# A two-layer trunk on one core: the stick-breaking stage gets a deeper pipeline, a half-height query tile and a GpSimd scaling

## The chip, the core and the metric

The program runs on one core of a Trainium2 chip, in one launch. What counts is the device time in microseconds (us). Before the change it is 1318.02 us, the median of 3 runs (1313.18, 1318.02 and 1321.62). The engines are TensorE (PE in the profile, with its weight loads as PEld), VectorE (DVE), ScalarE (ACT), GpSimd (POOL) and SyncE (SP), which issues most transfers.

## What is computed

The model has two layers on a sequence of 512 tokens of width 1024, all in float32. Layer 0 mixes with a gated delta net, layer 1 with stick-breaking attention; both also attend to 256 memory rows, and both end in an MLP. The change lies in two places: the stick-breaking attention of layer 1, and the softmax of the memory attention of both layers.

```python
def stick_breaking_attention(q, k, v):          # 12 heads of 64
    ...
        z = einsum('bthd,bshd->bhts', q[:, t0:t1], kb) * scale
        log_beta = log_sigmoid(z)
        log_1m_beta = where(before, log_sigmoid(-z), 0.0)
        tail = cumsum(log_1m_beta, axis=3, reverse=True) - log_1m_beta
        a = where(before, exp(log_beta + tail), 0.0)
        outs.append(einsum('bhts,bshd->bthd', a, vb))

def memory_attention(q, mem_kv):                # 4 heads of 64, 256 memory rows
    ...
    p = softmax(einsum('bshd,bmhd->bhsm', q, k) * X_HEAD_DIM ** -0.5, axis=-1)
    return einsum('bhsm,bmhd->bshd', p, v)
```

## The kernel before, in words

Every float32 matrix product is done with numbers that are split into a high part (fp32r) and the remainder, the low part; hi·hi, hi·lo and lo·hi are added up in one PSUM bank. ACT usually makes the high part by a copy, and DVE the low part by a subtraction (`split_lo`, L176).

The stick-breaking stage of layer 1 runs over *units*. A unit is one head and one entry of `BLOCKS = ((3, 2), (1,), (0,))`, that is one or two blocks of 128 keys against all queries that come later. There are 12 heads in 6 pairs, so 36 units; the two heads of a pair run one unit apart. `stick_breaking` is a generator that emits, in step n, the scores of unit n, the weights of unit n-`d1` and the value pass of unit n-`d2`:

- `sb_qk` projects query and key of a head in one product (128 output rows: 64 of q, 64 of k). From the PSUM bank ACT writes `qh` (q high, into both halves of the 128 partitions) and k high into the lower half of `kk`; DVE writes q low into both halves of `ql`, two instructions of 64x512 (L1075), and k low into the upper half of `kk`.
- `sb_scores` makes z in a bank `ps_g` by three products per block: `kk` with `qh` (L1092: k low and k high with q high in one pass over 128 rows), a mask (L1093, bf16), and `kk` with `ql` (L1095, also over 128 rows). ACT then forms log(1 + exp(-|z|)) in three instructions (L1100 to L1102), DVE adds max(z, 0) (L1103) and splits into `sp_h` (L1107) and `sp_l` (L176).
- `sb_weights` adds the reversed running sums to z by products of triangular and all-ones matrices with `sp_h` and `sp_l` (L1122). ACT takes exp into `sb_a` (L1125), DVE copies the high part `sb_ah` (L1128), and GpSimd subtracts for the low part `sb_al` (L1129).
- `sb_av` multiplies v with `sb_ah` and `sb_al` in a bank `ps_acc` (L1141), and folds the result into `mixT` when a head is complete.

Between the units the generator's caller places slices of the next pair's projection (`fm_slices`, L212) and, by the table `FILLN`, steps of `mem_attention`. There `scores` takes 256 tokens of one head at a time: two pairs of products (L691), a maximum on DVE (L694), two exponentials on ACT (L698), a reciprocal (L700) and the scaling of `p` by it, two instructions of 128x256 (L702); `turn` transposes `p` on PE (L711) and `values` multiplies with the memory values (L722). In layer 0 the same `mem_attention` is woven into the end of the delta net.

Each engine does its instructions strictly in the order in which they stand; the order comes from the framework's scheduler, which works on the emitted program, and from the pools: a new tile of a name with `bufs=k` waits until the one k before it has been read. The PSUM banks `ps_g` and `ps_acc` are four each.

Of the kernel before, what the change touches and what calls it, by code (L numbers as in the profile page):

```python
# [9 lines left out]
F32R = mybir.dt.float32r  # L10
I32 = mybir.dt.int32
BF16 = mybir.dt.bfloat16
AF = mybir.ActivationFunctionType
ALU = mybir.AluOpType
# [3 lines left out]
P = 128  # L18
S = 512
NT = S // P  # L20
D = 1024
# [3 lines left out]
W = H * DH  # L25
# [17 lines left out]
def f(ap):  # L43
    return ap.bitcast(F32)
# [23 lines left out]
class Trunk:  # L68
# [600 lines left out]
    def mem_attention(self, i, q, alloc, mixT):  # L669

        nc, v = self.nc, self.nc.vector
# [14 lines left out]
        def scores(h, t2):  # L686
# [14 lines left out]
            for j in range(2):  # L701
                v.tensor_scalar(out=p[:, j], in0=p[:, j], scalar1=sm[:, j:j + 1], scalar2=None, op0=ALU.mult)  # L702
# [359 lines left out]
    def sb_qk(self, pair, hi, lo, pool, out):  # L1062

        nc, v = self.nc, self.nc.vector
        top, low = slice(0, 64), slice(64, P)
        for hh in range(2):
            qh, ql, kk = (pool.tile([P, S], F32R, name=f"sb{n}", bufs=4) for n in ("qh", "ql", "kk"))
            out[hh] = (qh, ql, kk)

            def done(b):  # L1070
                nc.scalar.activation(out=qh[top], in_=b[top], func=AF.Copy, scale=0.125)
                nc.scalar.activation(out=kk[low], in_=b[low], func=AF.Copy)
                nc.scalar.activation(out=qh[low], in_=b[top], func=AF.Copy, scale=0.125)
                for o in (top, low):
                    v.scalar_tensor_tensor(out=ql[o], in0=b[top], scalar=0.125, in1=f(qh[top]), op0=ALU.mult,  # L1075
                                           op1=ALU.subtract)
                self.split_lo(kk[top], b[low], kk[low])
            yield from self.fm_slices(self.a["w_b_qk"][2 * pair + hh], hi, lo, done)

    def sb_scores(self, u, pool):  # L1080

        nc, v = self.nc, self.nc.vector
        qh, ql, kk = u["qk"][u["pr"].start // 64]
        u["zb"] = zb = self.bank("g")
        n = 0
        u["at"] = {}
        for i in u["blocks"]:
# [7 lines left out]
            nc.tensor.matmul(z, lhsT=kk[:, ks], rhs=ql[:, t0:], start=False, stop=True, skip_group_check=True)  # L1095
# [16 lines left out]
    def sb_weights(self, u, pool):  # L1112
# [13 lines left out]
        u["ah"] = pool.tile([P, S], F32R, name="sb_ah", bufs=2)[:, :n]  # L1126
        u["al"] = pool.tile([P, S], F32R, name="sb_al", bufs=2)[:, :n]
# [20 lines left out]
    def stick_breaking(self, qks, vv, pool, mixT):  # L1148
# [10 lines left out]
        d1, d2 = 2, 4  # L1159
# [173 lines left out]
def _qk_heads(w):  # L1333

    q, k = w[:, :W].reshape(D, 2 * H, 64), w[:, W:2 * W].reshape(D, 2 * H, 64)
    return np.concatenate([np.concatenate([q, k], 2).reshape(D, 2 * W), w[:, 3 * W:]], 1)
# [32 lines left out]
```

## Time and profile before

| | us |
|---|---|
| median of 3 runs | 1318.02 |
| the profiled execution, its own time | 1318.39 |
| span of that execution in the trace | 1316.7 |
| around the span | 1.7 |
| DVE busy / ACT busy / POOL busy | 861.8 / 717.5 / 163.9 |
| stick-breaking stage, first scores to last value pass | about 762 to 926 |

The page gives PE as busy for 97% of the span, but the ends of matmuls are modelled: a matmul of 512 columns is shown as 0.39 us long while the next begins 0.23 us after it. A busy PE therefore hides short stalls, and its idle time is a lower bound of what it loses. Stretches of time are read with the busy time of each engine in them; the stage of the change is cut at 833 us, where the memory attention of layer 1 has begun and PE stops being busy without a gap.

### The profile page before, as it was taken

To read this page: it belongs to the slowest core of one execution; us is meant where nothing else is said; L and a number is where in the kernel's file an instruction comes from. 1 tells how busy PE (TensorE), PEld (TensorE's weight loads), DVE (VectorE), ACT (ScalarE), POOL (GpSimd) and SP (SyncE) were. 2 spreads that over 40 slices of the span, in tenths; PEclk is the share of its full clock that TensorE was granted. 3 is DMA by queue.
4 is the path that set the end of the run, shared out by engine and by line. 5 is a ranking of instruction groups with operands and counts; after the bars stand their busy time and mean duration, and the time that the engine had idled before them with its cause. 6 is when DMAs were issued, how large, how long until landed. Compare 5 with 4: busy or idle time off the path is not lost.

```text
span 1316.7 us, 18097 instructions
## 1 busy us (share of the span) xinstructions
PE 1275.9 (97%) x6620; PEld 1070.0 (81%) x6620; DVE 861.8 (65%) x1588; ACT 717.5 (54%) x1378; POOL 163.9 (12%) x196
## 2 busy tenths in 40 slices
PE   7999999998999999999999999998999999999997
PEld 7788878887788888878888988786788888878886
DVE  7677695877663264555788678999573255455776
ACT  8654435446455454444565567878455344454561
POOL 2511313010021000000000013223130000000000
PEclk9999999999999999999999999999999999999999
DMA  7551654415689878644454426222679944544441
GB/s 242 192 166 58 161 130 117 123 51 143 210 245 266 233 190 243 195 145 143 148 186 139 157 75 150 76 64 64 208 255 256 257 127 144 148 141 150 152 144 64
DMA packets 82153, 209.39 MB, mean 159 GB/s; under 512 B 6720, under 2 KB 11840, under 8 KB 81616
## 3 DMA queue, kind: packets, MB, share of 16 engines
q1 hardware_dynamic: 62192, 164.12, 37.7%
q0 software_dynamic: 19296, 43.06, 16.4%
q8 instruction: 52, 0.85, 0.3%
q10 hardware_dynamic: 576, 1.05, 0.2%
q14 instruction: 37, 0.30, 0.1%
HBM read 199.29 MB, written 67.63 MB: 203 GB/s over the span
## 4 chain that ended last, share of the span: by engine, by line
PE 80%; DVE 10%; ACT 6%; issue 2%; DMA 1%; POOL 0%; SPq 0%; DVEq 0%; POOLq 0%; ACTq 0%
PE ps_acc L212 45%; PE ps_g L955 21%; PE ps_g L212 4%; PE ps_g L526 1%; PE ps_g L1122 1%; DVE wlo L176 1%; PE ps_g L389 1%; PE ps_g L518 1%; ACT whi L199 1%; PE ps_g L488 1%; ACT scrap L281 1%; DVE cv L360 1%; PE ps_g L295 1%; DVE sb_e L1103 1%; PE ps_acc L1141 1%
## 5 line engine op out<-in xcount | busy, mean ns | idle before, releaser
L212 PE MATMUL ps_acc<-h_hi,whi 128*128 128x512 f32 (+1 forms) x888 | 338.1, 381 | 0.0
L212 PE MATMUL ps_acc<-h_hi,wlo 128*128 128x512 f32 (+1 forms) x888 | 337.5, 380 | 0.0
L212 PE MATMUL ps_acc<-h_lo,whi 128*128 128x512 f32 (+1 forms) x888 | 335.1, 377 | 0.0
L176 DVE TENSOR_TENSOR wlo<-raw,whi 128x1024 fp32r<-128x1024 f32 x134 | 169.2, 1264 | 141.3 <-ACT whi L199 133.9
L955 PE MATMUL ps_g<-whi,sh 128*128 128x512 f32 x784 | 261.1, 395 | 0.0
L199 ACT ACTIVATE whi<-raw 128x1024 fp32r<-128x1024 f32 x134 | 141.8, 1059 | 203.0 <-PE ps_g L955 94.1
L176 DVE TENSOR_TENSOR wlo<-xc,whi 128x1024 fp32r<-128x1024 f32 x89 | 108.8, 1224 | 151.2 <-ACT whi L199 149.0
L212 PEld LDWEIGHTS ps_acc<-h_hi,wlo 128*128 128x128 f32 x888 | 167.5, 189 | 34.0 <-DVE wlo L176 3.9
L212 PEld LDWEIGHTS ps_acc<-h_hi,whi 128*128 128x128 f32 x888 | 167.8, 189 | 28.8 <-ACT whi L199 1.6
L212 PEld LDWEIGHTS ps_acc<-h_lo,whi 128*128 128x128 f32 x888 | 167.9, 189 | 28.4
L955 PEld LDWEIGHTS ps_g<-whi,sh 128*128 128x128 f32 x784 | 147.6, 188 | 34.5
L199 ACT ACTIVATE whi<-xc 128x1024 fp32r<-128x1024 f32 x89 | 94.3, 1060 | 137.1 <-PE ps_g L955 92.5
L955 PE MATMUL ps_g<-wlo,sh 128*128 128x512 f32 x392 | 154.8, 395 | 0.0
L955 PEld LDWEIGHTS ps_g<-wlo,sh 128*128 128x128 f32 x392 | 73.9, 189 | 17.2
L882 POOL DMA_DIRECT2D sum<-w_down x56 | 51.5, 1332 | 181.8 <-DMA sum<-w_down 104.4
L176 DVE TENSOR_TENSOR sh<-ua,sh 128x512 fp32r<-128x512 f32 x98 | 66.7, 685 | 4.7 <-ACT sh L936 4.7
L1129 POOL TENSOR_TENSOR sb_al<-sb_a,sb_ah 128x384 fp32r<-128x384 f32 (+1 forms) x36 | 41.2, 1144 | 154.8 <-DVE sb_ah L1128 133.1
L936 ACT ACTIVATE sh<-ua 128x512 fp32r<-128x512 f32 x98 | 59.9, 618 | 0.3
L212 PE MATMUL ps_acc<-ua 128*128 128x512 f32 x224 | 57.3, 391 | 0.0
L978 POOL DMA_DIRECT2D ua<-park x4 | 2.3, 574 | 388.6 <-DVE sh L176 381.2
L212 PEld LDWEIGHTS ps_acc<-ua 128*128 128x128 f32 x224 | 42.0, 188 | 8.9
L212 PE MATMUL ps_acc<-whi,h_hi 128*128 128x256 f32 (+1 forms) x144 | 44.5, 326 | 0.0
(352 smaller groups left out, 2148.2 us busy)
## 6 DMA issues: line engine op xcount, KB each, us to landing
sum<-w_down POOLq DMA_DIRECT2D x56, 512.0 KB, 9.9
xc<-w_up SPq DMA_DIRECT2D x38, 512.0 KB, 3.9
xc<-w_down SPq DMA_DIRECT2D x30, 512.0 KB, 3.9
xc<-sum SPq DMA_DIRECT2D x29, 512.0 KB, 4.0
sum<-w_down SPq DMA_DIRECT2D x28, 512.0 KB, 6.5
sum<-sum SPq DMA_DIRECT2D x28, 512.0 KB, 5.4
raw<-w_in_a SPq DMA_DIRECT2D x27, 512.0 KB, 3.8
raw<-sum SPq DMA_DIRECT2D x27, 512.0 KB, 3.7
```

Source lines behind the costliest of these rows:

```text
L176: self.nc.vector.tensor_tensor(out=lo, in0=src, in1=f(hi), op=ALU.subtract)
L199: self.nc.scalar.activation(out=hi, in_=raw, func=AF.Copy)
L212: self.nc.tensor.matmul(out, lhsT=l, rhs=r, start=start and k == 0 and i == 0, stop=stop and k == n - 1 and i == 2)
L281: nc.scalar.activation(out=self.scrap(m), in_=x[:, j * m:(j + 1) * m], func=AF.Square, accum_out=ssq[:, j:j + 1])
L295: op = nc.tensor.transpose(b[:, j, i * P:(i + 1) * P], xs[i][:, (kc + j) * P:(kc + j + 1) * P], self.ident)
L360: nc.vector.scalar_tensor_tensor(out=acc[:, j:], in0=b[:, :S - j], scalar=w[:, 3 - j:4 - j], in1=acc[:, j:], op0=ALU.mult, op1=ALU.add)
L389: self.nc.tensor.transpose(tp[:, t], src(t), self.ident)
L488: nc.tensor.matmul(sb[:, j], lhsT=self.sel[:, s4 + j], rhs=ud, start=True, stop=True)
L882: self.tc.keep_in_program_order(nc.gpsimd.dma_start(out=dst, in_=src, accum_op=ALU.add))
L936: nc.scalar.activation(out=s[:, 0], in_=src, func=AF.Copy)
L955: nc.tensor.matmul(y[t], lhsT=l, rhs=r, start=new and d == 0 and z == 0 and m == 0, stop=d == nd - 1 and z == 1 and m == 2, skip_group_che ...
L1129: nc.gpsimd.tensor_tensor(out=u["al"], in0=a, in1=f(u["ah"]), op=ALU.subtract)
```

## The change

Three edits are made, and the layout of the weights follows one of them.

- The value pass of a unit comes five steps behind its scores, not four (`d2`), and `sb_ah` and `sb_al` have three buffers each, not two.
- A pair's two heads share one tile `ql`: one head uses the upper 64 partitions, the other the lower ones. For the second head of a pair q and k change places in the weight's columns. The low part is written once, not twice, and the third product of the scores runs over 64 rows of `kk` and `ql` (`kk[kp, ks]`), where it ran over 128. Two pairs' `ql` tiles are kept, where four heads' were, so the memory that this frees is what the third `sb_ah` and `sb_al` take.
- The scaling of `p` in the memory attention (L702, both layers) is issued on GpSimd, not on DVE.

```diff
             for j in range(2):
-                v.tensor_scalar(out=p[:, j], in0=p[:, j], scalar1=sm[:, j:j + 1], scalar2=None, op0=ALU.mult)
+                nc.gpsimd.tensor_scalar(out=p[:, j], in0=p[:, j], scalar1=sm[:, j:j + 1], scalar2=None, op0=ALU.mult)
...
-        top, low = slice(0, 64), slice(64, P)
+        halves = slice(0, 64), slice(64, P)
+        ql = pool.tile([P, S], F32R, name="sbql", bufs=2)
         for hh in range(2):
-            qh, ql, kk = (pool.tile([P, S], F32R, name=f"sb{n}", bufs=4) for n in ("qh", "ql", "kk"))
-            out[hh] = (qh, ql, kk)
+            qh, kk = (pool.tile([P, S], F32R, name=f"sb{n}", bufs=4) for n in ("qh", "kk"))
+            qs, ks = halves[hh], halves[1 - hh]
+            out[hh] = (qh, ql[ks], kk, ks)
...
-                nc.scalar.activation(out=qh[top], in_=b[top], func=AF.Copy, scale=0.125)
-                nc.scalar.activation(out=kk[low], in_=b[low], func=AF.Copy)
-                nc.scalar.activation(out=qh[low], in_=b[top], func=AF.Copy, scale=0.125)
-                for o in (top, low):
-                    v.scalar_tensor_tensor(out=ql[o], in0=b[top], scalar=0.125, in1=f(qh[top]), op0=ALU.mult,
-                                           op1=ALU.subtract)
-                self.split_lo(kk[top], b[low], kk[low])
+                nc.scalar.activation(out=qh[qs], in_=b[qs], func=AF.Copy, scale=0.125)
+                nc.scalar.activation(out=kk[ks], in_=b[ks], func=AF.Copy)
+                nc.scalar.activation(out=qh[ks], in_=b[qs], func=AF.Copy, scale=0.125)
+                v.scalar_tensor_tensor(out=ql[ks], in0=b[qs], scalar=0.125, in1=f(qh[qs]), op0=ALU.mult,
+                                       op1=ALU.subtract)
+                self.split_lo(kk[qs], b[ks], kk[ks])
...
-            nc.tensor.matmul(z, lhsT=kk[:, ks], rhs=ql[:, t0:], start=False, stop=True, skip_group_check=True)
+            nc.tensor.matmul(z, lhsT=kk[kp, ks], rhs=ql[:, t0:], start=False, stop=True, skip_group_check=True)
...
-        u["ah"] = pool.tile([P, S], F32R, name="sb_ah", bufs=2)[:, :n]
-        u["al"] = pool.tile([P, S], F32R, name="sb_al", bufs=2)[:, :n]
+        u["ah"] = pool.tile([P, S], F32R, name="sb_ah", bufs=3)[:, :n]
+        u["al"] = pool.tile([P, S], F32R, name="sb_al", bufs=3)[:, :n]
...
-        d1, d2 = 2, 4
+        d1, d2 = 2, 5
...
     q, k = w[:, :W].reshape(D, 2 * H, 64), w[:, W:2 * W].reshape(D, 2 * H, 64)
-    return np.concatenate([np.concatenate([q, k], 2).reshape(D, 2 * W), w[:, 3 * W:]], 1)
+    qk = np.stack([q, k], 2)
+    qk[:, 1::2] = qk[:, 1::2, ::-1].copy()
+    return np.concatenate([qk.reshape(D, 2 * W), w[:, 3 * W:]], 1)
```

The order of instructions changes with it. First DVE, between two units of the fourth pair's time, before the change (the output's name stands left of the arrow, its inputs right of it; the numbers tell buffers apart):

```order
L1075 SCALAR_TENSOR_TENSOR sbql_8115<-ps_acc_8123,sbqh_8114 64x512 x2
L176 TENSOR_TENSOR sbkk_8116<-ps_acc_8123,sbkk_8116 64x512
L700 RECIPROCAL sm_8233<-sm_8233 128x2
L1128 CAST sb_ah_8266<-sb_a_8264 128x512
L702 TENSOR_SCALAR p_8234<-p_8234,sm_8233 128x256 x2
L1103 SCALAR_TENSOR_TENSOR sb_e_8247<-ps_g_8240,sb_e_8247 128x384
```

The same place on DVE with the change (its lines are two to four further down in the file):

```order
L1077 SCALAR_TENSOR_TENSOR sbql_8100<-ps_acc_8109,sbqh_8101 64x512
L176 TENSOR_TENSOR sbkk_8102<-ps_acc_8109,sbkk_8102 64x512
L700 RECIPROCAL sm_8215<-sm_8215 128x2
L1130 CAST sb_ah_8248<-sb_a_8246 128x512
L1148 TENSOR_TENSOR mixT_7144<-ps_acc_8048,sb_o_8254 64x512
L1105 SCALAR_TENSOR_TENSOR sb_e_8229<-ps_g_8222,sb_e_8229 128x384
```

One write of `sbql` and both scalings of `p` are gone from between the reciprocal and the next unit's `sb_e`; a fold into `mixT` has moved there. They stand now on GpSimd, whose queue before held only the subtractions for `sb_al` in this place:

```order
L1131 TENSOR_TENSOR sb_al_8188<-sb_a_8185,sb_ah_8187 128x384
L702 TENSOR_SCALAR p_8216<-p_8216,sm_8215 128x256 x2
L1131 TENSOR_TENSOR sb_al_8249<-sb_a_8246,sb_ah_8248 128x512
L1131 TENSOR_TENSOR sb_al_8297<-sb_a_8294,sb_ah_8296 128x384
L1131 TENSOR_TENSOR sb_al_8342<-sb_a_8339,sb_ah_8341 128x384
```

So the subtraction for `sb_al_8249` now stands behind two scalings that wait for the reciprocal on DVE. Last PE, the weights of one unit in the bank `ps_g_8681` and that unit's value pass (`sb_ah_8801`), before the change; rows in between that belong to other work are left out:

```order
L1122 MATMUL ps_g_8681<-sp_l2_8694,nones_r_332 128x128
L1122 MATMUL ps_g_8727<-sp_h0_8736,ntri_r_334 128x512
L1122 MATMUL ps_g_8780<-sp_h1_8789,ntri_r_334 128x384
L1141 MATMUL ps_acc_8900<-sb_ah_8801,v_6723 128x128
L1141 MATMUL ps_acc_8900<-sb_al_8802,v_6723 128x128
```

And the same with the change (bank `ps_g_8658`, value pass of `sb_ah_8778`):

```order
L1124 MATMUL ps_g_8658<-sp_l2_8671,nones_r_332 128x128
L1124 MATMUL ps_g_8707<-sp_h0_8716,ntri_r_334 128x512
L1124 MATMUL ps_g_8757<-sp_h1_8766,ntri_r_334 128x384
L1124 MATMUL ps_g_8798<-sp_h2_8810,ntri_r_334 128x128
L1143 MATMUL ps_acc_8916<-sb_ah_8778,v_6723 128x128
```

Between a unit's weights and its value pass there were the weights of two other units, and there are three now.

## Rows read from the trace of the kernel before

**Rows 1.** The page's first line.

```profile
span 1316.7 us, 18097 instructions
```

**Rows 2.** Busy time by stretch: stretch, length, each engine's busy us (instructions), granted clock, DMA.

```profile
762.00:833.00 71.00, 71.00 (x390) 59.89 (x389) 59.22 (x95) 53.88 (x99) 17.69 (x17) 1.00 0.48 121
833.00:926.00 93.00, 84.40 (x475) 68.04 (x474) 87.75 (x167) 73.08 (x161) 29.55 (x27) 1.00 0.22 56
```

**Rows 3.** Waits from 833 to 926 us: who waited for whom, us, times, longest.

```profile
PE ps_acc L1141 <- DVE sbkk L176: 2.3, 2, 1.2
PE ps_acc L1141 <- POOL sb_al L1129: 1.7, 3, 0.8
...
PE ps_acc L1141 <- DVE sb_ah L1128: 0.4, 2, 0.2
```

**Rows 4.** The chain of waits from 833 to 926 us, its shares by line.

```profile
by line: issue 9.5%; DVE sb_e L1103 8.1%; DVE sp_l L176 7.4%; DVE sp_h L1107 7.3%; DVE p L702 4.4%; ACT sb_e L1101 3.7%; ACT p L698 3.7%; ACT whi L199 3.6%; POOL sb_al L1129 3.6%; ACT sb_e L1100 3.6%; DVE sb_ah L1128 3.6%; PE ps_g L1122 3.5
```

**Rows 5.** DVE's groups from 833 to 926 us: busy us, mean ns of one, idle before.

```profile
L176 DVE TENSOR_TENSOR sp_l<-sb_e,sp_h 128x384 fp32r<-128x384 f32 x14 | 10.9, 778 | 0.2
...
L702 DVE TENSOR_SCALAR p<-p,sm 128x256 f32<-128x256 f32 x14 | 6.9, 532 | 0.1
L1075 DVE SCALAR_TENSOR_TENSOR sbql<-ps_acc,sbqh 64x512 fp32r<-64x512 f32 x10 | 6.8, 680 | 0.2
...
L1107 DVE CAST sp_h<-sb_e 128x384 fp32r<-128x384 f32 x14 | 6.4, 457 | 0.2
```

**Rows 6.** GpSimd's groups from 833 to 926 us, then one of the whole run.

```profile
L1129 POOL TENSOR_TENSOR sb_al<-sb_a,sb_ah 128x384 fp32r<-128x384 f32 x15 | 16.0, 1069 | 34.0 <-DVE sb_ah L1128 25.6 <-PE ps_acc L1141 3.7 <-ACT p L698 3.2
L1129 POOL TENSOR_TENSOR sb_al<-sb_a,sb_ah 128x512 fp32r<-128x512 f32 x8 | 10.8, 1350 | 30.4 <-DVE sb_ah L1128 30.4
...
L510 POOL MEMSET Q<- 128x256 f32 x18 | 6.9, 422 | 139.9 <-PE ps_g L526 137.0 <-DVE X L527 3.0
```

**Rows 7.** Timeline around 769 and 789 us, DVE and POOL: start us, length us, instruction.

```profile
769.85 0.56 DVE L176 TENSOR_TENSOR sp_l<-sb_e,sp_h 128x384 fp32r<-128x384 f32 x1
...
788.86 0.35 DVE L1107 CAST sp_h<-sb_e 128x384 fp32r<-128x384 f32 x1
789.24 1.58 DVE L176 TENSOR_TENSOR sp_l<-sb_e,sp_h 128x384 fp32r<-128x384 f32 x1
...
789.11 1.30 POOL L1129 TENSOR_TENSOR sb_al<-sb_a,sb_ah 128x512 fp32r<-128x512 f32 x1 [6.55 <-PE ps_acc L212]
```

**Rows 8.** The third product of the scores (L1095): all of it, then by stretch (PE, PEld).

```profile
L1095 PE MATMUL ps_g<-sbql,sbkk x48: 274/391/480, 762.7 to 910.2; 128*128 128x128 f32 x12, 128*128 128x256 f32 x12, 128*128 128x384 f32 x12, 128*128 128x512 f32 x12
...
833.00:926.00 93.00, 10.25 (x26) 5.19 (x26) 1.00 0.22 56
```

**Rows 9.** PE's timeline, around 763 us and around 284 us.

```profile
762.60 0.22 PE L1092 MATMUL ps_g<-sbqh,sbkk 128*128 128x128 f32 x1
762.66 0.23 PE L1093 MATMUL ps_g<-nmask,diag_bf 128*128 128x128 bf16 x1
762.70 0.30 PE L1095 MATMUL ps_g<-sbql,sbkk 128*128 128x128 f32 x1
762.85 0.33 PE L1092 MATMUL ps_g<-sbqh,sbkk 128*128 128x256 f32 x1
...
763.26 0.40 PE L212 MATMUL ps_acc<-h_hi,whi 128*128 128x512 f32 x1
763.49 0.39 PE L212 MATMUL ps_acc<-h_lo,whi 128*128 128x512 f32 x1
...
284.35 1.03 PE L389 MATMUL ps_g<-ident,X 128*128 128x128 f32 x8
285.14 0.37 PE L691 MATMUL ps_acc<-mk0h,qm 128*128 128x256 f32 x1
```

**Rows 10.** Layer 0's memory attention: a stretch, L702 alone on DVE, and its waits.

```profile
310.00:320.00 10.00, 8.38 (x56) 7.06 (x56) 7.73 (x23) 6.98 (x27) 0.61 (x1) 1.00 0.18 54
...
280.00:320.00 40.00, 4.88 (x16) 0.91 0.42 93
...
PE ps_acc L711 <- DVE p L702: 2.2, 3, 1.3
```

More of the change, by code (lines that the diff above doesn't have):

```diff
@@ L1082, in sb_scores @@
         nc, v = self.nc, self.nc.vector
-        qh, ql, kk = u["qk"][u["pr"].start // 64]
+        qh, ql, kk, kp = u["qk"][u["pr"].start // 64]
         u["zb"] = zb = self.bank("g")
```

## The prediction, made before the change was run

> **What bounds the kernel now.** I read first the busy time by stretch, then the waits in the stretch that loses time, then the chain of waits there, and last the groups of DVE and GpSimd. From 762 to 833 us PE is busy for the whole 71.00 us: this half of the stick-breaking stage is bound by PE, and nothing that DVE is spared can shorten it [rows 2]. From 833 to 926 us PE is busy for 84.40 of 93.00 us, so it idles for 8.6, while DVE is busy for 87.75 (94%) and ACT for 73.08 (79%). The reader is to see that DVE comes closest to being full there. The chain of waits agrees: the DVE lines that it names take 8.1 + 7.4 + 7.3 + 4.4 + 3.6 = 30.8% of the stretch, the ACT lines 3.7 + 3.7 + 3.6 + 3.6 = 14.6%, and PE's own work hardly shows [rows 4]. The gain is to be looked for in these 93 us, a fourteenth of the run, and its ceiling there is about the 8.6 us of idle PE.
>
> **DVE is spared.** Two things leave it in this stretch. The scaling of `p`, 14 instructions, is 6.9 us; of 10 writes of `ql` half go, 3.4 of 6.8 us [rows 5]. Together that is 10.3 us.
>
> **GpSimd is loaded, and DVE pays part of it.** The scaling has not run on GpSimd, so I bound it. A memset of 128x256, which only writes, took 0.422 us. The two forms of `sb_al`, with two inputs each, took 1.069 and 1.350 us for 384 and 512 columns; that is 0.28 us per 128 columns, so 256 columns would take 0.79 [rows 6]. One input lies between; I take 0.6, so 14 x 0.6 = 8.4 us (5.9 to 11.1). GpSimd is busy for 29.55 of the 93 us [rows 2] and has room. But a GpSimd instruction holds up DVE: `sp_l` of 128x384, which began 0.13 us after `sb_al`, took 1.58 us and ended 0.41 us after it [rows 7]. Early in the stage, with GpSimd idle, the same instruction took 0.56. On average it takes 0.778, and `sp_h` 0.457 against 0.35 with GpSimd idle [rows 5, 7]. That is 14 x 0.22 + 14 x 0.107 = 4.6 us lost to 26.8 us of `sb_al`, 0.17 us per us. The new scalings then cost DVE 8.4 x 0.17 = 1.4 us; the bounds are nothing and, were DVE to stand for all of their time, 11.1.
>
> **What of that reaches the end.** `p` alone is 4.4% of the chain, 4.1 us. Of the rest of DVE's work about a third is on the chain (30.8% of 93 is 28.6 us, of 87.75 busy), so `ql` brings 3.4 x 0.33 = 1.1 and the lost time takes 1.4 x 0.33 = 0.5. That makes 4.7 us. ACT, which gets no relief, is next: in the proportion of the two engines' shares of the chain, 30.8 to 14.6, I keep 68%, **3.2 us**.
>
> **The value pass one unit later.** PE waits at the value pass for `sb_al` 1.7 us in 3 waits and for `sb_ah` 0.4 us, never longer than 0.8 us at a time [rows 3]. The 48 score products span 147 us for 36 units [rows 8], so one unit more is 4.1 us of slack, and these **2.1 us** go. It also covers the new neighbours on GpSimd's queue, where a subtraction now stands behind two scalings (1.2 us) that wait for DVE's reciprocal. The 2.3 us at the same line that end with DVE's `sbkk` are a wait for a PSUM bank, not for the weights; they stay. What is late next is PE's wait for `sp_l`, whose distance (`d1`) does not change.
>
> **The narrower third product.** 48 products now run over 64 rows, between neighbours over 128, so TensorE changes its row setting 96 times: 44 times before 833 us, where each hundredth would show, and 52 times after [rows 8]. No row shows such a change. Below: the third product takes 0.15 us for 128 columns until the next starts, the first 0.06, because its weights' load is not hidden behind the mask's 0.04; if 64 rows saved that 0.09, the gain would be 4.3 us. Above: a matmul of 512 columns is shown as 0.40 us long and the next starts 0.23 after it; emptying the array each time would cost 0.17, 16 us in all. The nearest row is a change of kind: 8 transposes and then a product of another type take 0.79 us, 0.10 each as within a run, so that change is free [rows 9]. I take **zero**. The Trainium skill says otherwise (TensorEngine Tiling (Array Packing), Key Properties): a change of the tiling mode, not merely of the tile, drains the TensorE; no run here shows it, and by that rule the sum would come out as in the first rival below.
>
> **Work with one answer.** In layer 0, 16 scalings move off DVE (4.88 us), which is 77% busy where PE idles for 1.6 of 10 us; each then takes 0.3 us longer on a path on which PE already waited 2.2 us for `p` [rows 10]. The two cancel; I take zero, and 3 us either way for the range. ACT issues what it did. The shared `ql` tile is written while its pair's forerunner is finished with it, since both heads' last scores stand on PE ahead of the projection that fills it; were that not so, DVE would wait for one unit. The exchanged columns carry the same bytes in the same transfers. GpSimd's transfers (the sums for the MLP) now stand behind scalings, a few us later than before and far ahead of their readers. The third buffer costs no other tile its room.
>
> **Sum.** 3.2 + 2.1 = 5.3 us less than the profiled execution. That took 1318.39 us (span 1316.7 [rows 1] and 1.7 around it), 0.4 above the median, so 1313.1, or **1313** against the runs. Chance 0.45, own range 1306 to 1317.
>
> **Rivals.**
> - *Row settings cost.* Each of the 96 changes empties the array, 0.17 us. Before 833 us, where PE has no idle time, 44 x 0.17 = 7.5 us come on top. After it 52 x 0.17 = 8.8 us of new PE time fill the 8.6 of idle, so that the relief brings nothing. That is 1318.4 + 7.5 = **1326**, slower than before. It decides from 5.3 / 44 = 0.12 us per change if the later ones hide, and from 5.3 / 96 = 0.055 if none does. For it speaks that no product of the kernel has had fewer than 128 rows, and the page named above; against it that a change of kind is free [rows 9]. Chance 0.25.
> - *GpSimd takes it back.* The scalings take 0.79 us and DVE stands for all of it: 11.1 us against 10.3 spared. Only the later value pass is left, 2.1 us: **1316**. For it: the 1.58 us of `sp_l` [rows 7]. Against: on average 0.17, not 1. Chance 0.15.
> - *All idle time goes.* DVE was the only cause; 8.6 us in the stretch and 1.6 in layer 0 [rows 10]: 10.2 less, **1308**. For it: 94% of DVE [rows 2]; against: ACT stays at 79%, and the bank and `sp_l` waits stay. Chance 0.10.
> - *It does not do what it says.* The waits at the value pass are for banks, and ACT takes DVE's place at once: **1318**. Chance 0.05.
>
> **Range and chances.** One per cent is 13 us, about what a measurement of this kernel can tell from no change (its three runs lie 8.4 us apart). The range runs from 1304, the case that all idle goes less the 3 us that layer 0 may bring, to 1327, just above the row-setting case. Faster by over 1% (below 1304.8) needs more than all idle time of the stretch, or stalls that the modelled matmuls hide: 0.10. Slower by over 1% (above 1331.2) needs the row changes to cost more than an emptied array, the weights' load for instance: 0.09. Within 1%: 0.81.
>
> **What would show it.** Right: from 833 us to the end of the stage 5 us fewer, PE idle there about 3 us; DVE below 90%; waits for `sb_al` and `sb_ah` at the value pass gone, those for banks and `sp_l` left; no DVE group L702. The row settings are seen in the timeline where the third product follows the mask and where the next product follows it: starts 0.04 and 0.15 us later (128 columns) mean no price. GpSimd's share is seen in the mean of its L702 group, 0.6 us, and in `sp_l` and `sp_h`, which should stay near 0.8 and 0.46. I am wrong if the half before 833 us gets longer, or if the later half keeps its length although DVE is free.

## The result: 1.2% slower, and the profile after

The changed kernel takes **1334.92 us**, the median of 6 runs (1334.49 to 1337.40), against 1320.74 for the kernel before on the same chip, again of 6 runs. The ratio, estimated from all these runs, is **1.0117**, 95% interval 1.0098 to 1.0135 (the two medians alone give 1.0107). The forecast was 1313, with a range to 1327; it is wrong in size and in sign. The profiled execution spans 16.1 us more than the one before [rows 1], the first line of the page after:

```profile
span 1332.8 us, 18120 instructions
```

Where these 16.1 us lie is read from landmarks. The row below is the MLP's product L955 of the changed kernel; the two times at the end are its first and last start. Before they were 465.5 and 1297.3 us.

```profile
L955 PE MATMUL ps_g<-whi,sh x784: 389/393/404, 472.2 to 1313.4; 128*128 128x512 f32 x196
```

So 6.7 us are lost before the first L955, that is in layer 0 (two kernels below that change nothing there still come 3 us later than the kernel before, so this number is good to some 3 us). From the first scores (762.6 before, 769.3 after) to the last start of a value pass (925.5 and 941.7) the stick-breaking stage takes 172.4 us, where it took 162.9: **9.5 us more**. Behind it nothing differs (371.8 and 371.7 us to the last L955).

**The stick-breaking stage.** Busy time by stretch of the changed kernel, in the columns of [rows 2]:

```profile
769.00:840.00 71.00, 70.91 (x352) 56.20 (x351) 51.06 (x79) 49.80 (x89) 16.41 (x16) 1.00 0.41 104
840.00:942.00 102.00, 96.93 (x510) 76.34 (x509) 87.61 (x154) 78.62 (x172) 47.97 (x44) 1.00 0.21 57
```

PE is as full as before in the first 71 us and issues 352 instructions in them, not 390. In the rest its idle time has gone down, from 8.6 to 5.1 us, and DVE is 86% busy and no longer 94%; yet the stretch is 9 us longer, because the 71 us ahead of it now hold fewer blocks. So the halves are better cut at the same block. These rows count the last 26 of the 48 blocks of scores by their first product, in the kernel before and in the changed one, with the first and last start:

```profile
L1092 PE MATMUL ps_g<-sbqh,sbkk x26: 221/337/477, 833.1 to 909.9; 128*128 128x384 f32 x7, 128*128 128x512 f32 x7, 128*128 128x128 f32 x6, 128*128 128x256 f32 x6
L1094 PE MATMUL ps_g<-sbqh,sbkk x26: 220/384/474, 847.0 to 924.6; 128*128 128x384 f32 x7, 128*128 128x512 f32 x7, 128*128 128x128 f32 x6, 128*128 128x256 f32 x6
```

The first 22 blocks take 77.7 us (769.3 to 847.0), where they took 70.5: **7.2 us more**, with PE idle for no more than 0.1 us. From there to the last value pass it is 94.7 us, where it was 92.4: 2.3 more. The larger part of the loss lies where PE was full before.

In the later part PE has become the bound too, which the chain of waits from 840 to 942 us says at once (shares by line; before, the lines of DVE led it [rows 4]):

```profile
by line: PE ps_acc L212 19.6%; PE ps_g L1124 12.3%; PE ps_acc L1143 6.6%; issue 6.3%; PE ps_g L1097 4.8%; DVE sb_e L1105 4.1%; DVE sp_l L176 4.1%; POOL sb_al L1131 3.3%; DVE sp_h L1109 3.0%; PE ps_g L1094 2.7%; ACT p L698 2.4%; ACT sb_e L11
```

What PE does longer stands in its timeline at the first two blocks of scores (start, length, instruction), which answers to [rows 9]:

```profile
769.30 0.22 PE L1094 MATMUL ps_g<-sbqh,sbkk 128*128 128x128 f32 x1
769.37 0.23 PE L1095 MATMUL ps_g<-nmask,diag_bf 128*128 128x128 bf16 x1
769.53 0.32 PE L1097 MATMUL ps_g<-sbql,sbkk 64*128 64x128 f32 x1
769.78 0.38 PE L1094 MATMUL ps_g<-sbqh,sbkk 128*128 128x256 f32 x1
770.00 0.23 PE L1095 MATMUL ps_g<-nmask,diag_bf 128*128 128x128 bf16 x1
770.16 0.38 PE L1097 MATMUL ps_g<-sbql,sbkk 64*128 64x256 f32 x1
770.47 0.50 PE L212 MATMUL ps_acc<-h_hi,whi 128*128 128x512 f32 x1
770.81 0.39 PE L212 MATMUL ps_acc<-h_lo,whi 128*128 128x512 f32 x1
```

From mask to narrow product it is 0.16 us, where it was 0.04; from the narrow product of 128 columns to the next one 0.25, where it was 0.15; and the product behind that is itself late in releasing its successor (770.00 - 769.78 = 0.22 against 0.17, 770.81 - 770.47 = 0.34 against 0.23). Two blocks and the first product after them take 1.51 us, where they took 0.89: **0.31 us for each block**. With 48 blocks that is 14.9 us, or 0.155 for each of 96 changes; 22 blocks make 6.8 of it, about the 7.2 that the first part is longer.

**Layer 0.** The 16 scalings on GpSimd (duration in ns as minimum, median and maximum, then first and last start), and the wait for them that PE has at the transposes:

```profile
L702 POOL TENSOR_SCALAR p<-p,sm x16: 913/925/1448, 293.7 to 320.6; 128x256 f32<-128x256 f32 x16
```

```profile
PE ps_acc L711 <- POOL p L702: 5.7, 8, 1.5
```

On DVE one took 0.346 us, 16 were issued within 19.4 us (293.7 to 313.1), and PE waited 2.2 us for them in 3 waits [rows 10]. Now one takes 0.925, the 16 stretch over 26.9 us, 7.5 more, and PE waits at each of the 8 units.

### The profile page after: what moved, and what is told of

Its sections match the earlier page's. It is cut to its first block, busy times and chain, and to the rows that moved or that the text cites. A ratio compares the mean times of both kernels' runs of the same rounds, so it can differ in the third digit from the quotient of the medians.

```text
span 1332.8 us, 18120 instructions
## 1 busy us (share of the span) xinstructions
PE 1291.5 (97%) x6620; PEld 1076.2 (81%) x6620; DVE 850.8 (64%) x1544; ACT 719.0 (54%) x1378; POOL 196.4 (15%) x228
## 3 DMA queue, kind: packets, MB, share of 16 engines
q0 software_dynamic: 19296, 43.06, 16.1%
## 4 chain that ended last, share of the span: by engine, by line
PE 83%; DVE 8%; ACT 4%; issue 2%; POOL 1%; DMA 1%; DVEq 0%; POOLq 0%; ACTq 0%
PE ps_acc L212 46%; PE ps_g L955 21%; PE ps_g L212 4%; PE ps_g L1124 2%; PE ps_g L518 1%; PE ps_g L526 1%; PE ps_g L389 1%; DVE wlo L176 1%; ACT whi L199 1%; PE ps_g L1097 1%; PE ps_acc L1143 1%; PE ps_g L488 1%; POOL p L702 1%; PE ps_g L295 1%; DVE cv L360 1%
## 5 line engine op out<-in xcount | busy, mean ns | idle before, releaser
L212 PE MATMUL ps_acc<-h_hi,whi 128*128 128x512 f32 (+1 forms) x888 | 338.8, 382 | 0.1
L212 PE MATMUL ps_acc<-h_hi,wlo 128*128 128x512 f32 (+1 forms) x888 | 337.1, 380 | 0.0
L212 PE MATMUL ps_acc<-h_lo,whi 128*128 128x512 f32 (+1 forms) x888 | 335.1, 377 | 0.0
L955 PE MATMUL ps_g<-whi,sh 128*128 128x512 f32 x784 | 261.1, 395 | 0.0
L212 PEld LDWEIGHTS ps_acc<-h_hi,wlo 128*128 128x128 f32 x888 | 167.5, 189 | 34.0 <-DVE wlo L176 3.6
L212 PEld LDWEIGHTS ps_acc<-h_hi,whi 128*128 128x128 f32 x888 | 167.8, 189 | 30.2 <-ACT whi L199 1.6
L212 PEld LDWEIGHTS ps_acc<-h_lo,whi 128*128 128x128 f32 x888 | 167.9, 189 | 28.1
L955 PEld LDWEIGHTS ps_g<-whi,sh 128*128 128x128 f32 x784 | 147.6, 188 | 34.5
L955 PE MATMUL ps_g<-wlo,sh 128*128 128x512 f32 x392 | 154.8, 395 | 0.0
L955 PEld LDWEIGHTS ps_g<-wlo,sh 128*128 128x128 f32 x392 | 73.9, 189 | 17.2
L212 PE MATMUL ps_acc<-ua 128*128 128x512 f32 x224 | 57.2, 391 | 0.0
L212 PEld LDWEIGHTS ps_acc<-ua 128*128 128x128 f32 x224 | 42.0, 188 | 8.9
L212 PE MATMUL ps_acc<-whi,h_hi 128*128 128x256 f32 (+1 forms) x144 | 44.5, 326 | 0.0
```

Source lines behind the costliest of these rows:

```text
L212: self.nc.tensor.matmul(out, lhsT=l, rhs=r, start=start and k == 0 and i == 0, stop=stop and k == n - 1 and i == 2)
L955: nc.tensor.matmul(y[t], lhsT=l, rhs=r, start=new and d == 0 and z == 0 and m == 0, stop=d == nd - 1 and z == 1 and m == 2, skip_group_che ...
```

## The experiments

Theory **T1** after this reading: two prices, the row changes of TensorE (0.31 us a block) and the scaling on GpSimd in layer 0, less what the change recovers in the stage. The rivals: GpSimd caused all of it, the clock did, the narrow product is not dearer, the fifth unit costs by itself. Ratios are to the kernel before, run on the same chip in turn; one thousandth is 1.3 us. The runs of one kernel spread with TensorE's granted clock: the kernel before took 1313.04 us in a run with a mean clock of 0.999 and 1319.59 in one with 0.993, so a thousandth of the clock is worth about 1 us (an estimate). Where two kernels differ in it, the text says so.

| kernel | edit in short | median us | ratio, 95% interval |
|---|---|---|---|
| changed kernel | | 1334.92 | 1.0117, 1.0098 to 1.0135 |
| x1 | before + narrow product | 1325.87 | 1.0051, 1.0030 to 1.0071 |
| x2 | before + scaling on GpSimd | 1326.84 | 1.0049, 1.0030 to 1.0068 |
| x3 | before + lo parts written once | 1317.75 | 0.9988, 0.9974 to 1.0001 |
| x4 | changed, four units | 1334.51 | 1.0111, 1.0091 to 1.0131 |
| x5 | changed, layer 0 on DVE | 1326.48 | 1.0058, 1.0039 to 1.0076 |
| x6 | changed, both layers on DVE | 1326.18 | 1.0049, 1.0031 to 1.0067 |
| x7 | changed, narrow products side by side | 1332.18 | 1.0104, 1.0084 to 1.0123 |
| x8 | x6 with four units | 1329.21 | 1.0069, 1.0049 to 1.0090 |
| x9 | before + half of layer 0's scalings on GpSimd | 1318.64 | 0.9991, 0.9979 to 1.0003 |
| x10 | no third product, four units | 1307.88 | 0.9917, 0.9903 to 0.9930 |
| x11 | no third product, five units | 1313.83 | 0.9952, 0.9933 to 0.9971 |
| x12 | x3 with x9 | 1318.40 | 0.9999, 0.9983 to 1.0015 |

### x1: the narrow product alone

```diff
-            nc.tensor.matmul(z, lhsT=kk[:, ks], rhs=ql[:, t0:], start=False, stop=True, skip_group_check=True)
+            nc.tensor.matmul(z, lhsT=kk[64:, ks], rhs=ql[64:, t0:], start=False, stop=True, skip_group_check=True)
```

> The kernel before, with one edit: the third score product of each of the 48 blocks contracts over the 64 rows of the key hi part alone (it leaves out the product of the two lo parts, nothing else). Theory T1 (the changed kernel lost time in two places: about 0.31 us of TensorE per 128-64-128 row change, and the scaling on GpSimd in layer 0): 22 blocks lie in the stretch in which PE is never idle, 22 x 0.31 = 6.8 us; the 26 of the later stretch add 26 x 0.31 = 8.1 us, less what fits into PE's 8.6 us of idle time there. So 7 to 12 us slower, 1324 to 1329 against 1317, and no change before the first scores. Rival R1 (GpSimd and its contention with VectorE caused the whole loss): no change, within 2 us. Rival R2 (the narrower product is cheaper): up to 4 us faster.

Measured 1.0051, that is 6.7 us (4.0 to 9.4). R1 and R2 fall; T1's two prices hold, its 7 to 12 being a little high. The stage from first scores to last value pass, in two stretches:

```profile
765.70:836.70 71.00, 71.00 (x354) 56.80 (x353) 55.00 (x86) 49.94 (x90) 16.34 (x16) 1.00 0.42 104
836.70:936.30 99.60, 96.11 (x505) 75.07 (x503) 91.92 (x174) 77.61 (x171) 30.23 (x28) 1.00 0.23 61
```

PE is busy 167.1 us in it, against 154.9 in the same landmarks of the kernel before (762.0 to 925.5), and idle for 3.5, against 8.6. So 12.2 us of work came and 5.1 us of idle time went, **without DVE being spared anything**. Cut at the same block, the first 22 blocks take 77.4 us, 6.9 more than before, and the rest 93.2, 0.8 more: where PE had no idle time the whole price shows, behind it nearly nothing. A stage that PE stretches gives the other engines time, and its stalls close by themselves. That is the half of the result that T1 did not have: what the rest of the change was to recover had already gone.

### x2: the scaling on GpSimd alone

```diff
-                v.tensor_scalar(out=p[:, j], in0=p[:, j], scalar1=sm[:, j:j + 1], scalar2=None, op0=ALU.mult)
+                nc.gpsimd.tensor_scalar(out=p[:, j], in0=p[:, j], scalar1=sm[:, j:j + 1], scalar2=None, op0=ALU.mult)
```

> The kernel before, with one edit: the scaling of the memory weights on GpSimd in both layers. T1: 5 to 8 us slower before the first L955 (layer 0), and between 2 us faster and 2 us slower in the stick-breaking stage, where 32 operations of 0.3 us leave a busy VectorE but GpSimd's other work there waits: 1320 to 1327 in all. Rival R1 (GpSimd caused the whole loss): 14 to 18 us slower, 1331 to 1335, of it 9 in the stick-breaking stage. Rival R3 (layer 0's loss comes from where the clock fell, not from the scaling): no change in layer 0, within 2 us in all.

Measured 1.0049, 6.5 us: in all as T1 expects. The first L955 comes at 475.7 us, 10.2 later than before, which is more than T1's 5 to 8. The stage takes 164.0 us against 162.9, so GpSimd neither ruins it (R1 falls) nor helps it, although DVE's busy time in it falls from 146.7 to 143.9. The wait at layer 0's transposes is back, and in one stretch a lower clock with it:

```profile
PE ps_acc L711 <- POOL p L702: 5.2, 8, 1.5
```

```profile
290.00:300.00 10.00, 6.40 (x41) 5.64 (x42) 6.55 (x15) 5.55 (x18) 4.76 (x6) 0.85 0.08 29
300.00:310.00 10.00, 8.90 (x45) 8.22 (x44) 4.86 (x14) 4.47 (x15) 4.59 (x6) 0.64 0.00 0
310.00:320.00 10.00, 9.21 (x38) 8.16 (x39) 4.04 (x11) 4.12 (x14) 3.98 (x5) 0.53 0.56 105
```

The granted clock of 0.53 from 310 to 320 us is near the lower of PE's two levels (1.2 of 2.4 GHz); PE had idled for 3.6 of the 10 us in which it began to fall. The kernel before shows such a fall too (0.66 from 290 to 300 us); the changed kernel has 0.85 from 290 to 300 and 0.63 from 300 to 310. So the clock has a part in the loss of both in layer 0, and a larger one in x2, whose runs have a mean clock of 0.9897 where the kernel before has 0.9934: by the estimate above more than half of the 6.5 us. Whether the longer waits bring the clock down is not shown.

### x3: the lo parts written once, without a row change

```diff
+        k.qls = [[sp.tile([P, S], F32R, name=f"sbql{i}{j}") for j in range(2)] for i in range(2)]
+        for i in range(2):
+            for j in range(2):
+                nc.gpsimd.memset(f(k.qls[i][j])[(slice(0, 64), slice(64, P))[j]], 0.0)
...
-        ql = pool.tile([P, S], F32R, name="sbql", bufs=2)
+            ql = self.qls[pair % 2][hh]
...
-            nc.tensor.matmul(z, lhsT=kk[kp, ks], rhs=ql[:, t0:], start=False, stop=True, skip_group_check=True)
+            nc.tensor.matmul(z, lhsT=kk[:, ks], rhs=ql[:, t0:], start=False, stop=True, skip_group_check=True)
```

> The changed kernel with three parts undone: scaling on VectorE, value pass four units behind with two sets of weights, and the third product over all 128 rows again. For that each head has its own query lo tile, whose other half is set to zero once. What stays is that a query lo part is written once and not twice (24 operations of VectorE fewer). T1: no row changes, no slow scaling, so the recovered stalls alone show: 3 to 5 us faster than the kernel before, 1312 to 1314. Rival R4 (the saved VectorE work is worth nothing, since other waits close the gap): within 1.5 us of the kernel before. Rival R1 also expects about 3 us faster here, since nothing is on GpSimd.

Measured 0.9988 (0.9974 to 1.0001): 1.6 us faster, and between nothing and 3.4. That is less than T1's 3 to 5 and nearer to R4. The stage takes 162.6 us, 0.3 less than before. Its later part shows why: DVE is spared 3 us of 87.5, and PE's idle time falls by 1.5 us only, to 7.0. The first two blocks and the product behind them take 0.89 us here (starts at 765.31 and 766.20), as in the kernel before, so the exchanged columns cost nothing. x1, which has neither these nor the shared tile, pays 1.51 us in the same place (765.72 and 767.23): the price is that of the 64 rows.

```profile
836.30:927.90 91.60, 84.56 (x474) 67.61 (x473) 84.52 (x157) 73.50 (x161) 28.20 (x27) 1.00 0.21 56
```

### x4: the changed kernel with four units

```diff
-        u["ah"] = pool.tile([P, S], F32R, name="sb_ah", bufs=3)[:, :n]
-        u["al"] = pool.tile([P, S], F32R, name="sb_al", bufs=3)[:, :n]
+        u["ah"] = pool.tile([P, S], F32R, name="sb_ah", bufs=2)[:, :n]
+        u["al"] = pool.tile([P, S], F32R, name="sb_al", bufs=2)[:, :n]
...
-        d1, d2 = 2, 5
+        d1, d2 = 2, 4
```

> The changed kernel with the value pass four units behind the scores again and two sets of weights. T1: the fifth unit was worth something: 1 to 3 us slower than the changed kernel, 1.013 to 1.015 of the kernel before. Rival R5 (the longer distance or its third set of weights costs time, by banks or by memory): 2 us or more faster than the changed kernel, 1.010 or less.

Measured 1.0111, against 1.0117: no difference that can be told. Neither T1's 1 to 3 us nor R5 is shown. The clock is not equal either (0.9897 on average in x4's runs, 0.9915 in the changed kernel's), which leans towards five units by some 2 us. (In its profile the granted clock is 0.95 from 840 to 945 us, so its stage of 175.9 us isn't compared.)

### x5 and x6: the scaling back on DVE in layer 0, then in both layers

```diff
-                nc.gpsimd.tensor_scalar(out=p[:, j], in0=p[:, j], scalar1=sm[:, j:j + 1], scalar2=None, op0=ALU.mult)
+                (v, nc.gpsimd)[i].tensor_scalar(out=p[:, j], in0=p[:, j], scalar1=sm[:, j:j + 1], scalar2=None, op0=ALU.mult)
```

In x6 `v` stands in place of the choice by layer `i`.

> The changed kernel with the scaling of layer 0 back on VectorE, that of layer 1 still on GpSimd. T1: layer 0's loss goes, 5 to 8 us less than the changed kernel, that is 1.005 to 1.008 of the kernel before; what is left is all in the stick-breaking stage. Rival R1 (GpSimd beside VectorE in the stage is what costs): no more than 2 us less than the changed kernel, 1.010 or more. Rival R3 (layer 0's loss is the clock's, not the scaling's): no change, 1.011 or more.

> The changed kernel with the scaling of both layers back on VectorE; narrow third product, three sets and five units stay. T1, mended by the first four runs (a stage lengthened by the row changes hides its stalls by itself, so that the spared VectorE work and the fifth unit have nothing left to recover): 1.004 to 1.007 of the kernel before, as the narrow product alone (1.0051), and PE idle in the stage near 4 us. Rival R6 (the spared work and the fifth unit still recover their 5 us beside the row changes): 1.000 to 1.002. Rival R1 (scaling on GpSimd relieves VectorE in the stage): slower than the version with layer 1 on GpSimd by over 1 us.

Measured 1.0058 and 1.0049. Layer 0 back on DVE gives 0.0059 back, 7.8 us, with an uncertainty of some 3.5. Not all of it is the scaling's waits: the mean clock is 0.9952 in x5's runs and 0.9915 in the changed kernel's, which makes nearly half of it by the estimate above, so R3 may hold in part. Layer 1 then makes no difference beyond the uncertainty in the medians. The profiles tell more, for the stage is repeated within 0.1 us by kernels that do the same in it (162.9 and 162.8 us in the kernel before and x9, 172.4 and 172.5 in the changed kernel and x5): it takes 170.1 us in x6, so layer 1's scaling on GpSimd costs some 2.4 us there, far less than R1 needs, and is not the relief of DVE that the prediction counted on. The first L955 starts at 464.2 us in x5 and 467.6 in x6; in x1, x3, x8, x10 and x11, with layer 0 on DVE too, at 468.6, 468.3, 464.2, 469.5 and 467.8. In the four kernels with it on GpSimd (changed, x2, x4, x7) it starts at 472.2, 475.7, 472.0 and 472.8. The groups don't overlap, though 464 and 468 differ among kernels that do the same. And x6, with the lo parts written once and five units, is no better than x1 without both (1.0051), as the mended T1 has it and R6 has not. Its stage:

```profile
764.60:835.60 71.00, 70.90 (x351) 56.10 (x349) 51.24 (x80) 49.92 (x90) 16.41 (x16) 1.00 0.42 104
835.60:934.70 99.10, 96.40 (x506) 75.42 (x504) 86.09 (x168) 76.85 (x171) 29.86 (x28) 1.00 0.21 56
```

PE idles for 2.8 us, 0.7 less than in x1, for 9.6 us less of DVE's work (137.3 against 146.9). That is what the relief is worth here.

### x7: is it the change that costs, or the narrow product?

```diff
-            nc.tensor.matmul(z, lhsT=kk[kp, ks], rhs=ql[:, t0:], start=False, stop=True, skip_group_check=True)
             n += S - t0
+        for i in u["blocks"]:
+            t0 = i * P
+            nc.tensor.matmul(zb[:, u["at"][i]], lhsT=kk[kp, t0:t0 + P], rhs=ql[:, t0:], start=False, stop=True,
+                             skip_group_check=True)
```

> The changed kernel with one edit: in the twelve units that have two blocks the two narrow products stand one behind the other, so that TensorE goes from 128 to 64 rows and back 36 times and not 48, with the same 48 narrow products. T1 (the price is that of a change, about 0.25 to 0.31 us for there and back): 12 x 0.25 to 12 x 0.31 = 3.0 to 3.7 us of PE time less, of which 1 to 3.5 us show, 1.009 to 1.011 of the kernel before; in the timeline the second narrow product starts without the 0.11 us that the instruction behind a change waits. Rival R7 (the price is that of a narrow product, whatever stands before it): no change, 1.0117, and the second narrow product is as late as the first.

The time, 1.0104 (1.0084 to 1.0123), lies where T1 puts it, but its interval holds the changed kernel's 1.0117 too. The timeline decides:

```profile
769.86 0.22 PE L1094 MATMUL ps_g<-sbqh,sbkk 128*128 128x128 f32 x1
769.93 0.23 PE L1095 MATMUL ps_g<-nmask,diag_bf 128*128 128x128 bf16 x1
769.97 0.36 PE L1094 MATMUL ps_g<-sbqh,sbkk 128*128 128x256 f32 x1
770.17 0.23 PE L1095 MATMUL ps_g<-nmask,diag_bf 128*128 128x128 bf16 x1
770.33 0.49 PE L1100 MATMUL ps_g<-sbql,sbkk 64*128 64x128 f32 x2
770.75 0.50 PE L212 MATMUL ps_acc<-h_hi,whi 128*128 128x512 f32 x1
771.09 0.40 PE L212 MATMUL ps_acc<-h_lo,whi 128*128 128x512 f32 x1
```

The same two blocks and the product behind them take 1.23 us; with all 128 rows it was 0.89, with two changes there and back 1.51. One trip there and back costs 0.34, two cost 0.62, so the second narrow product, standing behind a narrow one, adds next to nothing (R7 falls). The price is that of the change.

### x8: x6 with four units

The edit is that of x4, made on x6.

> The changed kernel with the scaling of both layers on VectorE and the value pass four units behind with two sets. T1, mended: the fifth unit is worth nothing beside the row changes, within 1.5 us of the version with five units, 1.004 to 1.007 of the kernel before, and no more than 1.5 us from the narrow product alone (1.0051), since the lo parts written once are worth nothing there either. Rival R6: 2 to 4 us slower than the version with five units.

Measured 1.0069, against 1.0049 for x6: 2.6 us in favour of the fifth unit, with an uncertainty of some 3.7. Undecided between the two; the mean with x4, where it cost 0.8, is a gain of 0.9 us, give or take 2.6. The clock alone could make the 2.6 (0.9915 on average in x8's runs, 0.9946 in x6's).

### x9: one of each two scalings on GpSimd

```diff
-                v.tensor_scalar(out=p[:, j], in0=p[:, j], scalar1=sm[:, j:j + 1], scalar2=None, op0=ALU.mult)
+                (v, nc.gpsimd)[j * (1 - i)].tensor_scalar(out=p[:, j], in0=p[:, j], scalar1=sm[:, j:j + 1], scalar2=None, op0=ALU.mult)
```

> The kernel before, with one edit: in layer 0 the second of each pair of scalings goes to GpSimd, the first stays on VectorE; layer 1 as before. Theory T1 (what costs in layer 0 is the time from the reciprocal to the end of the second scaling, since TensorE waits for it at each of 8 transposes): on VectorE that is 2 x 0.35 = 0.70 us, on GpSimd 2 x 0.93 = 1.86, split 0.93 or 0.23 more than before, 8 x 0.23 = 1.8 us; so 0 to 3 us slower than the kernel before, 1.000 to 1.002. Rival R8 (any trip over GpSimd, with its signals, or GpSimd's occupation costs): at least half of the loss of the version with both on GpSimd, 3 us or more, 1.0025 or more.

Measured 0.9991 (0.9979 to 1.0003). The trip over GpSimd costs nothing that shows; R8 falls. PE's wait for `p` at the transposes is 2.3 us in 3 waits, as before.

```profile
L702 DVE TENSOR_SCALAR p<-p,sm x24: 340/353/1418, 295.5 to 921.6; 128x256 f32<-128x256 f32 x24
L702 POOL TENSOR_SCALAR p<-p,sm x8: 912/942/1081, 295.6 to 314.4; 128x256 f32<-128x256 f32 x8
```

Eight scalings of 0.942 us lie here from 295.6 to 314.4 us, 18.8 us, as the 16 did on DVE (19.4). One slow scaling beside a fast one is hidden; two in a row (1.85 us from the reciprocal to the transposes, where it was 0.69) are not.

### x10 and x11: the fifth unit where PE has less to do

```diff
-            nc.tensor.matmul(z, lhsT=kk[kp, ks], rhs=ql[:, t0:], start=False, stop=True, skip_group_check=True)
...
-                v.scalar_tensor_tensor(out=ql[ks], in0=b[qs], scalar=0.125, in1=f(qh[qs]), op0=ALU.mult,
-                                       op1=ALU.subtract)
```

The depth alone, on top of x3, was not tried, since x3's four full `ql` tiles take the memory of the third `sb_ah` and `sb_al`. So the third product was left out of both; they do less than is asked and serve the comparison alone.

> The changed kernel without the third product and the query lo parts (they are left out), scaling on VectorE, value pass four units behind. It is the ground for the next kernel: TensorE has about 11 us less to do in the stage than before (48 products of 0.15 to 0.31 us), so its waits are laid open. 4 to 9 us faster than the kernel before, 0.993 to 0.997, with more than 8.6 us of idle PE in the stage.

> The kernel just named (it leaves out the same), with the value pass five units behind and three sets of weights. T1, mended (the fifth unit is worth what PE idles at the value pass, and beside the row changes there was nothing to idle): here 1 to 4 us faster than with four units, 0.001 to 0.003 lower in ratio. Rival R9 (the fifth unit only moves the waits to the next product): within 1 us of it.

Both expectations missed. With four units the kernel takes 0.9917, more than the 4 to 9 us, and PE idles in the stage for 5.0 us, not for more than 8.6. With five it is **4.6 us slower** than with four (0.9952 against 0.9917, an uncertainty of some 3.1): the fifth unit neither helps nor only moves the waits. Their stages, at a clock of 1.00 in both, take 153.4 and 156.8 us, and PE idles for 5.0 and 10.0 of them. The stage of x10, then of x11:

```profile
766.50:837.50 71.00, 71.00 (x387) 59.51 (x386) 53.60 (x90) 56.48 (x107) 18.68 (x18) 1.00 0.45 119
837.50:920.00 82.50, 77.49 (x430) 61.80 (x428) 76.01 (x149) 70.39 (x154) 28.05 (x26) 1.00 0.24 63
```

```profile
764.80:835.80 71.00, 68.73 (x373) 57.21 (x372) 53.77 (x88) 54.99 (x101) 18.85 (x18) 1.00 0.47 119
835.80:921.60 85.80, 78.06 (x437) 62.64 (x435) 76.72 (x148) 71.28 (x159) 27.38 (x26) 1.00 0.20 51
```

And the wait that is new in x11, the largest of its stage; x10 has none of that kind:

```profile
PE ps_acc L212 <- DVE sbkk L176: 5.3, 4, 1.7
```

The next pair's projection (L212) waits for a `ps_acc` bank until DVE has read `sbkk` from it. The value pass takes its bank out of the same four, so one unit later moves it to another place in their rotation; that this is why the projection now falls on a bank just in use is argued from the wait and was not tested.

### x12: the two that came out just below the kernel before

x3 with the edit of x9.

> The two versions that came out just below the kernel before, together: each query lo part written once into a tile of 128 rows whose other half is zero (scaling on VectorE in layer 1, four units, two sets), and in layer 0 the second of each pair of scalings on GpSimd. T1, mended: the two ratios, 0.9988 and 0.9991, multiply to 0.998; the spared writes are worth 0 to 3 us in the stage, the split 0 or a little more: 1313 to 1319, with an interval that may just leave 1. Rival R4 (neither part is worth anything): 0.999 to 1.001. Both expect it well below the changed kernel (1.0117).

Measured 0.9999 (0.9983 to 1.0015). R4 is nearer than T1, but the clock is 0.9923 on average in x12's runs and 0.9943 in those of the kernel before beside them, so a gain of some 2 us is not excluded. No version with the third product is shown to beat the kernel before, and none is slower than the changed kernel.

## Why the prediction was wrong, point by point

- **The narrower third product is the step that failed.** It was taken as zero, from the nearest row, a change of kind between transposes and a product of another type that cost nothing. That row doesn't change the rows in use, and was no neighbour. The price is 0.31 us for a trip there and back (the timeline, x7), 0.155 a change. The first rival had put 0.17 on it, 16 us in all, close to the 14.9 here, and with its 1326 it is just what x1 (1325.87) and x6 (1326.18) measure. Its split holds too: 7.5 us on top where PE never idled (6.9 in x1, 7.2 in the changed kernel), and the later changes hidden (0.8 in x1). The sign of being wrong that the prediction named first, a longer half before 833 us, is what came. That rival should have been the forecast: its upper bound came from a mechanism, the zero from a row of another kind. The trace agrees with the rule of the Trainium skill named in the prediction (TensorEngine Tiling (Array Packing), Key Properties), that a change of tiling mode drains TensorE, in that a change has a price, 0.31 us for both ways. Whether it is an emptied array or a weight load that no longer runs ahead is open. The load for the product behind a narrow one, in the kernel before and then in the changed one:

```profile
763.14 0.19 PEld L212 LDWEIGHTS ps_acc<-h_hi,whi 128*128 128x128 f32 x1
770.47 0.19 PEld L212 LDWEIGHTS ps_acc<-h_hi,whi 128*128 128x128 f32 x1
```

  It began 0.12 us ahead of its product (763.26) and now begins with it (770.47).
- **Layer 0 is the second.** The sum had "0.3 us longer each on a path on which PE already waited" and cancelled it against the relief of DVE. A scaling takes 0.58 us longer (0.925 against 0.346), there are two in a row before PE may go on, and PE waits at all 8 units, 5.7 us and not 2.2. With the lower clock of these runs, which may make nearly half of it, the loss is 7.8 us (the changed kernel against x5). The cancelling had no ground: what DVE is spared lies beside the path, the scaling on it.
- **GpSimd's price** was taken at 0.6 us with bounds of 0.42 and 0.79; it was 0.925 in layer 0 and 1.054 on average in the stage, outside both. The upper bound assumed that a one-input operation can't cost more than a two-input one of the same columns. It does:

```profile
L702 POOL TENSOR_SCALAR p<-p,sm 128x256 f32<-128x256 f32 x16 | 16.7, 1054 | 20.2 <-DVE sm L700 19.1 <-ACT sb_e L1104 1.1
L1131 POOL TENSOR_TENSOR sb_al<-sb_a,sb_ah 128x384 fp32r<-128x384 f32 x15 | 16.2, 1082 | 19.2 <-DVE sb_ah L1130 14.2 <-PE ps_acc L212 5.0
```

  These are GpSimd's groups of the changed kernel from 840 to 942 us [rows 6]: 256 columns with one input take about as long as 384 with two.
- **That GpSimd holds up DVE little** was right. `sp_l` and `sp_h` of 384 columns, forecast to stay near 0.8 and 0.46 us [rows 5], did, with 48 us of GpSimd beside them and not 30:

```profile
L176 DVE TENSOR_TENSOR sp_l<-sb_e,sp_h 128x384 fp32r<-128x384 f32 x14 | 11.2, 799 | 0.4
...
L1109 DVE CAST sp_h<-sb_e 128x384 fp32r<-128x384 f32 x14 | 6.0, 429 | 0.3
```

- **What the relief of DVE brings** (3.2 us) was read from DVE's share of the chain. The relief came (138.5 us busy in the stage, 146.7 before), the gain did not: for `p` the stage gets longer, by 1.1 us in x2 and 2.4 in x5 against x6; for `ql` x3 shows 0.3 in the stage and 1.6 (0 to 3.4) in all, where the step had 1.1. Beside the row changes nothing is left to gain, since x1 loses its stalls without any relief.
- **The value pass one unit later** (2.1 us) was wrong in its size and, where PE has less to do, in its sign (x11). The sum also had no term for the end of the stage: from the last scores to the last value pass it takes 15.6 us with four units (the kernel before and x1) and 17.3 with five (x6). In the changed kernel the waits for `sb_ah` went, those for `sb_al` did not [rows 3], for GpSimd now also scales (with the scaling on DVE, in x6, they are 0.8 us in one wait):

```profile
PE ps_acc L1143 <- POOL sb_al L1131: 1.7, 2, 1.3
```

- **The sum of the parts.** Narrow product 6.7, GpSimd 6.5, lo parts -1.6: 11.6 us, against 15.4 (12.9 to 17.8) for the whole. The 3.8 us between are within the uncertainties of the four, some 4.7 together. The stage shows that at least one part hurts the others: layer 1's scaling on GpSimd costs 1.1 us of it alone (x2) and 2.4 beside the rest (x5 against x6).
- **The range.** Its lower end was to be 1308 less 3 us, which is 1305 and not 1304; nothing hangs on it.

## What to carry to other kernels

Halving an operand to the rows that it needs is not free: between products of full height each trip to 64 rows and back costs 0.31 us, so fill the other half with zeros, or put narrow products side by side. An engine's relief is worth only the idle time of the bound that it closes, and if the same change gives the bound more work, that idle time closes by itself. And work goes to a slower engine only where nobody waits for its end: count the operations in a row between two signals (2 x 0.93 us cost 7.8 us in layer 0, a lower clock included; 1 x 0.94 beside a fast one cost nothing).

## What the hardware showed that was not expected

- A row change is paid in three places: 0.12 us before the narrow product, 0.10 to 0.11 behind it, and 0.05 to 0.11 more until the product after that has released the next.
- GpSimd's scaling of 128x256 by one number a row takes 0.925 us, 2.7 times DVE's 0.346, and 3.6 ns a column against 2.8 for its subtraction of two inputs (1.08 us for 384). The Trainium skill (GPSIMD Engine Reference, Engine selection) has one-input operations roughly at line rate; for this one the trace says otherwise, and the measurement decides.
- A pipeline one unit deeper can cost time without any new work: PE idles for 5.0 us more in x11's stage than in x10's, and 5.3 us of waits for a PSUM bank are new in it.
